# MLP products of a two-layer trunk with both activation parts as one 512-column moving operand

## Chip, cores and metric

The kernel runs on one core of a Trainium2 chip. The metric is the device time of one execution in microseconds (us). The profiler records one execution; times of instructions come from it.

## What is computed

The input is 256 tokens of width 2048 and there are two layers. A layer has a mixer part (input projection, retention, forgetting attention, mLSTM, output projection) and an MLP. The change touches the MLP:

```python
h = rmsnorm(x, norm_mlp_w[layer]) * (1.0 + sc_m) + sh_m
x = x + g_m * (jnp.square(jax.nn.relu(h @ w_ff1[layer])) @ w_ff2[layer])
```

`w_ff1` is 2048 x 8192 and `w_ff2` is 8192 x 2048, all in float32. `sh_m`, `sc_m` and `g_m` come from a matrix-vector product of a condition with `ada_w` (the "ada" work below).

## The kernel before

**Layout.** Activations lie transposed: a tile holds 128 features on the partitions and the 256 tokens along the free axis. The normalised input of a layer part is 16 such tiles (k = 0 to 15).

**Products in parts.** A float32 product is made of three products of rounded parts. A weight tile w is split into a high part wh (a cast on ACT, L221) and a low part wl = w - wh (a subtraction on DVE or POOL, L227); activations are split the same way into hh and hl (L499, L500), and the product is the sum of wh x hl, wl x hh and wh x hh. In `mm_b` (L252 to L254) the weight part is the stationary operand (128 x 128) and an activation part is the moving operand (256 columns), so each pair of k and 128-column block n takes three matmuls with three weight loads, all into the same 256 columns of PSUM. This document calls such a group of three a triple. In `mm_a` (L263 to L265), which makes the v, g and o blocks of the input projection, the activations are stationary and 512 weight columns move.

**Weights.** `chunk` loads a 4 x 128 x 512 piece of a weight matrix as two DMAs of 128 x 1024 values (512 KB each, six buffers `raw`), and `split` makes wh and wl of each (three buffers each). A tile therefore holds two k by four n. `pool_share` is the share of the low parts made on POOL: 0.3 and 0.8 in the two passes of the first ff1 stage of layer 0, 0.8 in the rest of its MLP, and 0 in layer 1.

**PSUM.** `pair` gives a tile of 1024 columns (two banks); there are two of them. An ff1 or ff2 block of 512 outputs fills one pair: four n of 256 columns.

**The MLP.** `ff1` makes a block of 512 hidden features from 16 k tiles. ACT evicts it with a relu (L964), squares it (L969) and casts it to the high part (L971); DVE makes the low part (L972). `ff2` takes two such blocks (8 k tiles) at a time and adds four output blocks of 512 to x, each evicted by four DVE instructions (`residual`, L796). The program order is ff1 of step s, then ff2 of step s - 1, for s = 0 to 7. In layer 0 the first six ff1 blocks are made in two passes over 8 k each (the partial sum is kept in SBUF, L952 and L960), because the modulation of the upper k tiles comes later. The first block of a layer's ff1 is a "lead" (`lead`, L471 to L473): it uses 258 columns of an unnormalised input, so that it can start ahead of the norm. The last output block of layer 1 is made in four small pieces (`ff2_tail`).

**Order of the work.** Each engine and SP's DMA queue runs its instructions in a fixed order that a scheduler with a timeline model chose. The ada work is spread over the MLP by `step`: each ada tile is two DMAs and two DVE products of 128 x 1024 (L283), so that in layer 0 weight DMAs and ada DMAs alternate in SP's queue, and DVE's order mixes ada products with subtractions and evictions.

The lines that the change and the prediction touch:

```python
out += [(hi[:, i, :], lo[:, i, :]) for i in range(step)]          # chunk: a tile holds 2 k x 512 columns
nc.tensor.matmul(o, lhsT=wh[:, s], rhs=al, ...)                   # mm_b, three per (k, n)
nc.tensor.matmul(o, lhsT=wl[:, s], rhs=ah, ...)
nc.tensor.matmul(o, lhsT=wh[:, s], rhs=ah, ...)
```

## Time and profile before

| what | value |
|---|---|
| median of 3 runs | 2548.88 us (2541.46 to 2551.96) |
| the profiled execution | 2549.75 us |
| its span, first to last instruction | 2548.0 us |
| mean granted TensorE clock | 0.977 |
| instructions | 46455 |

Time around the span is 2549.75 - 2548.0 = 1.75 us. In the profile PE is the matmul, PEld the weight load, DVE is VectorE, ACT is ScalarE, POOL is GpSimd, and SP issues the DMAs. Matmuls are pipelined: a matmul's own duration overlaps the next one's, so the cost of one matmul in a stream is the distance from its start to the next start. "Granted clock" 1.00 is TensorE at 2.4 GHz.

### The profile page before, as it was taken

To read this page: it belongs to the slowest core of one execution; us is meant where nothing else is said; L and a number is where in the kernel's file an instruction comes from. 1 tells how busy PE (TensorE), PEld (TensorE's weight loads), DVE (VectorE), ACT (ScalarE), POOL (GpSimd) and SP (SyncE) were. 2 spreads that over 40 slices of the span, in tenths; PEclk is the share of its full clock that TensorE was granted. 3 is DMA by queue.
4 is the path that set the end of the run, shared out by engine and by line. 5 is a ranking of instruction groups with operands and counts; after the bars stand their busy time and mean duration, and the time that the engine had idled before them with its cause. 6 is when DMAs were issued, how large, how long until landed. Compare 5 with 4: busy or idle time off the path is not lost.

```text
span 2548.0 us, 46455 instructions
## 1 busy us (share of the span) xinstructions
PE 2450.1 (96%) x19016; PEld 2378.3 (93%) x19016; DVE 1583.2 (62%) x2427; ACT 1180.9 (46%) x1442; POOL 758.9 (30%) x314
## 2 busy tenths in 40 slices
...
GB/s 359 299 327 329 305 217 265 285 299 338 322 334 310 279 288 297 287 280 298 285 213 241 272 247 266 192 166 178 178 182 186 188 182 183 187 185 183 186 187 91
DMA packets 177246, 630.45 MB, mean 247 GB/s; under 512 B 19588, under 2 KB 24326, under 8 KB 177032
## 3 DMA queue, kind: packets, MB, share of 16 engines
...
q10 hardware_dynamic: 432, 0.39, 0.1%
...
## 4 chain that ended last, share of the span: by engine, by line
PE 79%; DVE 9%; DMA 4%; issue 3%; POOL 3%; ACT 2%; SPq 0%; DVEq 0%; POOLq 0%; ACTq 0%
PE pj L253 23%; PE pj L252 23%; PE pj L254 23%; DMA ada<-ada_w 3%; POOL wl L227 3%; DVE ada L283 2%; PE pj L264 2%; PE pj L265 2%; PE pj L263 2%; DVE wl L227 2%; PE mx L620 1%; ACT wh L221 1%; DVE cv L709 1%; DVE blk L437 0%; DMA raw<-ada_w 0%
## 5 line engine op out<-in xcount | busy, mean ns | idle before, releaser
L221 ACT CAST wh<-raw 128x1024 fp32r<-128x1024 f32 x804 | 840.4, 1047 | 1129.8 <-PE pj L254 881.3
L227 POOL TENSOR_TENSOR wl<-raw,wh 128x1024 fp32r<-128x1024 f32 (+1 forms) x309 | 756.3, 2451 | 583.4 <-ACT wh L221 565.3
L227 DVE TENSOR_TENSOR wl<-raw,wh 128x1024 fp32r<-128x1024 f32 x495 | 615.7, 1246 | 487.4 <-ACT wh L221 486.7
L252 PE MATMUL pj<-hl,wh 128*128 128x256 f32 x2912 | 830.9, 286 | 9.5 <-DVE hl L500 8.2
L253 PE MATMUL pj<-hh,wl 128*128 128x256 f32 x2912 | 830.4, 285 | 7.2 <-DVE wl L227 7.2
L254 PE MATMUL pj<-hh,wh 128*128 128x256 f32 x2912 | 828.1, 284 | 0.0
L253 PE MATMUL pj<-blk,wl 128*128 128x256 f32 x2528 | 713.6, 282 | 6.6 <-DVE wl L227 5.2
L252 PE MATMUL pj<-blk,wh 128*128 128x256 f32 x2528 | 712.8, 282 | 2.8 <-ACT blk L538 1.5
L254 PE MATMUL pj<-blk,wh 128*128 128x256 f32 x2528 | 711.3, 281 | 0.0
L283 DVE SCALAR_TENSOR_TENSOR ada<-ada,cond 128x1024 f32<-128x1024 f32 x380 | 456.7, 1214 | 227.7 <-DMA ada<-ada_w 225.6
L252 PEld LDWEIGHTS pj<-hl,wh 128*128 128x128 f32 x2912 | 561.8, 193 | 10.7 <-DVE hl L500 8.9
L253 PEld LDWEIGHTS pj<-hh,wl 128*128 128x128 f32 x2912 | 562.4, 193 | 9.3 <-DVE wl L227 8.7
L254 PEld LDWEIGHTS pj<-hh,wh 128*128 128x128 f32 x2912 | 562.1, 193 | 0.2
L253 PEld LDWEIGHTS pj<-blk,wl 128*128 128x128 f32 x2528 | 478.5, 189 | 7.3 <-DVE wl L227 5.6
L252 PEld LDWEIGHTS pj<-blk,wh 128*128 128x128 f32 x2528 | 478.8, 190 | 3.4 <-ACT blk L538 1.9
L254 PEld LDWEIGHTS pj<-blk,wh 128*128 128x128 f32 x2528 | 479.3, 190 | 0.0
L1045 POOL TENSOR_TENSOR blk<-blk,R 128x1024 f32<-128x1024 f32 x1 | 2.4, 2357 | 1199.1 <-ACT R L405 1199.1
L264 PE MATMUL pj<-wl,hh 128*128 128x512 f32 x384 | 155.4, 405 | 8.5 <-DVE wl L227 8.4
L796 DVE SCALAR_TENSOR_TENSOR X<-pj,mod,X 128x256 f32<-128x256 f32 x284 | 117.8, 477 | 64.0 <-PE pj L254 63.9
L263 PE MATMUL pj<-wh,hl 128*128 128x512 f32 x384 | 153.2, 399 | 1.2 <-ACT wh L221 1.2
L265 PE MATMUL pj<-wh,hh 128*128 128x512 f32 x384 | 152.9, 398 | 0.0
L264 PEld LDWEIGHTS pj<-wl,hh 128*128 128x128 f32 x384 | 73.7, 192 | 24.5 <-DVE wl L227 10.7
...
## 6 DMA issues: line engine op xcount, KB each, us to landing
...
```

The costliest lines, as they stand in the source:

```text
L221: nc.scalar.copy(hi, raw)
L227: eng.tensor_tensor(lo, raw, hi.bitcast(F32), ALU.subtract)
L252: nc.tensor.matmul(o, lhsT=wh[:, s], rhs=al, start=st, stop=False, skip_group_check=True)
L253: nc.tensor.matmul(o, lhsT=wl[:, s], rhs=ah, start=False, stop=False, skip_group_check=True)
L254: nc.tensor.matmul(o, lhsT=wh[:, s], rhs=ah, start=False, stop=last, skip_group_check=True)
L263: nc.tensor.matmul(o, lhsT=al[:, s], rhs=wh, start=first, stop=False)
L264: nc.tensor.matmul(o, lhsT=ah[:, s], rhs=wl, start=False, stop=False)
L265: nc.tensor.matmul(o, lhsT=ah[:, s], rhs=wh, start=False, stop=last)
L283: nc.vector.scalar_tensor_tensor(raw, raw, 1.0, self.cond, ALU.mult, ALU.mult, accum_out=self.part[l][:, i, h:h + 1])
L620: nc.tensor.matmul(ps[:, i * P:i * P + P], lhsT=lt, rhs=v[:, j, c:c + P], start=first, stop=last, skip_group_check=True)
L709: V.scalar_tensor_tensor(y[:, s:], x[:, n, :T - s], w[:, 3 - s:4 - s], y[:, s:], ALU.mult, ALU.add)
L796: V.scalar_tensor_tensor(self.X(k), ps[:, n * T:n * T + T], self.mod[l][:, c:c + 1], self.X(k), ALU.mult, ALU.add)
```

## The change

The high and low parts of the activations become one tile, `h[:, k]` (or the two halves of a hidden tile), so that wh meets both in one matmul of 512 columns, and wl meets the high part in one of 256 columns. The 512-column result lies in one PSUM bank as two halves, wh x high (+ wl x high) and wh x low, which are added at eviction. A pair of banks now holds two n instead of four. `w_ff1` and `w_ff2` are laid out in blocks of 256 columns; a weight tile is one DMA of four k by 256 columns, of the same size as before. relu and square become one DVE instruction. The lead takes its weights from two such tiles per four k.

```diff
--- before.py
+++ after.py
@@ -116,8 +116,7 @@
     def constants(self):
         nc, c, io = self.nc, self.const, self.io
         self.Xq = [self.acts.tile([P, 4, T], F32, name=f"X{i}") for i in range(4)]
-        self.hh = self.acts.tile([P, KT, T], F32R, name="hh")
-        self.hl = self.acts.tile([P, KT, T], F32R, name="hl")
+        self.h = self.acts.tile([P, KT, 2, T], F32R, name="h")
         self.vec = c.tile([P, DEPTH * NVEC + KT], F32, name="vec")
         nc.scalar.dma_start(self.vec, io["vec"])
         crow = c.tile([2, 1024], F32, name="crow")
@@ -241,6 +240,31 @@
             out += [(hi[:, i, :], lo[:, i, :]) for i in range(step)]
         return out
 
+    def chunk2(self, src):
+
+        raw = self.raw.tile([P, 4, 256], F32, tag="raw", name=self.name("raw"))
+        self.wdma.append(self.nc.sync.dma_start(raw, src))
+        hi, lo = self.split(raw, 4, 256)
+        return [(hi[:, i, :], lo[:, i, :]) for i in range(4)]
+
+    def mm_w(self, ps, w, act, first, last):
+
+
+        nc = self.nc
+        wh, wl = w
+        for n in range(2):
+            s = slice(n * P, n * P + P)
+            o = ps[:, n * 512:n * 512 + 512]
+            nc.tensor.matmul(o.rearrange("p (a b) -> p a b", b=T), lhsT=wh[:, s], rhs=act, start=first, stop=False,
+                             skip_group_check=True)
+            nc.tensor.matmul(o[:, :T], lhsT=wl[:, s], rhs=act[:, 0, :], start=False, stop=last, skip_group_check=True)
+
+    @staticmethod
+    def sums(ps):
+
+        v = ps.rearrange("p (n c) -> p n c", c=512)
+        return v[:, :, 0:T], v[:, :, T:2 * T]
+
     def mm_b(self, ps, w, act, first, last):
 
         nc = self.nc
@@ -457,25 +481,37 @@
             if c == stat_at[1]:
                 self.stat_spread(aux)
             nk = min(4, kts[-1] + 1 - k0)
-            w = self.chunk(wsrc(k0, nk), nk)
+            w = wsrc(k0, nk)
             if js == 3:
                 self.step(nk / 4)
             for k in range(k0, k0 + nk):
                 if k not in self.U:
                     self.lead_u(l, js, jc, [k, k + 1])
-                (wh, wl), (uh, ul) = w[k - k0], self.U.pop(k)
+                uh, ul = self.U.pop(k)
                 f, e = k == kts[0], k == kts[-1]
                 for n in range(4):
-                    s = slice(n * P, n * P + P)
+                    wh, wl = w(k - k0, n)
                     o = ps[n][:, :LT]
-                    nc.tensor.matmul(o, lhsT=wh[:, s], rhs=ul, start=f, stop=False)
-                    nc.tensor.matmul(o, lhsT=wl[:, s], rhs=uh, start=False, stop=False)
-                    nc.tensor.matmul(o, lhsT=wh[:, s], rhs=uh, start=False, stop=e)
+                    nc.tensor.matmul(o, lhsT=wh, rhs=ul, start=f, stop=False)
+                    nc.tensor.matmul(o, lhsT=wl, rhs=uh, start=False, stop=False)
+                    nc.tensor.matmul(o, lhsT=wh, rhs=uh, start=False, stop=e)
         if self.r is None:
             self.stat_sum(aux)
         if self.R is None:
             self.stat_spread(aux)
         return ps
+
+    def lead_win(self, l):
+        def get(k, nk):
+            w = self.chunk(self.io["w_in"][l, 0, k // 4][:, k % 4:k % 4 + nk, :], nk)
+            return lambda i, n: tuple(x[:, n * P:n * P + P] for x in w[i])
+        return get
+
+    def lead_ff1(self, l):
+        def get(k, nk):
+            w = [self.chunk2(self.io["w_ff1"][l, b, k // 4]) for b in range(2)]
+            return lambda i, n: tuple(x[:, n % 2 * P:n % 2 * P + P] for x in w[n // 2][i])
+        return get
 
     def lead_out(self, ps, dst, func=AF.Identity, scale=1.0):
         nc = self.nc
@@ -496,11 +532,12 @@
                 s = js * KT + k + i
                 nc.scalar.activation(t[:, i, :], t[:, i, :], AF.Identity,
                                      scale=self.mod[l][:, c:c + 1], bias=self.mod[l][:, s:s + 1])
-            nc.scalar.copy(self.hh[:, k:k + 2, :], t)
-            nc.vector.tensor_tensor(self.hl[:, k:k + 2, :], t, self.hh[:, k:k + 2, :].bitcast(F32), ALU.subtract)
+            hi, lo = self.h[:, k:k + 2, 0, :], self.h[:, k:k + 2, 1, :]
+            nc.scalar.copy(hi, t)
+            nc.vector.tensor_tensor(lo, t, hi.bitcast(F32), ALU.subtract)
 
     def hact(self, k):
-        return self.hh[:, k, :], self.hl[:, k, :]
+        return self.h[:, k, 0, :], self.h[:, k, 1, :]
 
 
     def gate_mm(self, l):
@@ -842,7 +879,7 @@
             self.pump_until(l, 0, kts[-1])
             led = g == 0 and cfg["lead_win"]
             if led:
-                ps = self.lead(l, 0, 1, lambda k, n: io["w_in"][l, 0, k // 4][:, k % 4:k % 4 + n, :], kts, cfg["stat_win"])
+                ps = self.lead(l, 0, 1, self.lead_win(l), kts, cfg["stat_win"])
             if l > 0:
                 self.h_make(l, 0, 1, kts)
             if led:
@@ -911,15 +948,13 @@
             led = g == 0
             self.rate(cfg["ada_ff1"][g], nb * len(kts) / 4)
             if led:
-                ps = self.lead(l, 3, 4, lambda k, n: io["w_ff1"][l, 0, k // 4][:, k % 4:k % 4 + n, :], kts, cfg["stat_ff1"])
+                ps = self.lead(l, 3, 4, self.lead_ff1(l), kts, cfg["stat_ff1"])
             self.h_make(l, 3, 4, kts)
             if led:
                 acc[0] = self.slot()
+                self.lead_out(ps, acc[0])
                 if kts[-1] == KT - 1:
-                    self.lead_out(ps, acc[0], AF.Relu)
                     acc[0] = self.square(acc[0])
-                else:
-                    self.lead_out(ps, acc[0])
             for b in range(1 if led else 0, nb):
                 acc[b] = self.ff1(l, b, kts, acc.get(b))
         self.pool_share = cfg["pool_ff"]
@@ -937,63 +972,63 @@
 
     def ff1(self, l, b, kts, acc=None):
         nc = self.nc
-        ps = self.pair()
-        for k0 in range(kts[0], kts[-1] + 1, 4):
-            nk = min(4, kts[-1] + 1 - k0)
-            r0 = k0 % 4
-            w = self.chunk(self.io["w_ff1"][l, b, k0 // 4][:, r0:r0 + nk, :], nk)
-            for i in range(nk):
-                k = k0 + i
-                self.mm_b(ps, w[i], self.hact(k), k == kts[0], k == kts[-1])
-            self.step(nk / 4)
-        if kts[-1] != KT - 1:
-            if acc is None:
-                acc = self.slot()
-                nc.scalar.copy(self.flat(acc), ps)
+        done = kts[-1] == KT - 1
+        fresh = acc is None
+        t = self.slot() if fresh else acc
+        for h in range(2):
+            ps = self.pair()
+            for k0 in range(kts[0], kts[-1] + 1, 4):
+                w = self.chunk2(self.io["w_ff1"][l, 2 * b + h, k0 // 4])
+                for k in range(k0, k0 + 4):
+                    self.mm_w(ps, w[k - k0], self.h[:, k], k == kts[0], k == kts[-1])
+                self.step(0.5)
+            d = t[:, 2 * h:2 * h + 2, :]
+            p0, p1 = self.sums(ps)
+            if fresh:
+                nc.scalar.copy(d, p1)
             else:
-                d = self.flat(acc)
-                nc.vector.tensor_tensor(d, ps, d, ALU.add)
-            return acc
-        if acc is not None:
-            t = acc
-            d = self.flat(t)
-            nc.vector.tensor_tensor(d, ps, d, ALU.add)
-            nc.scalar.activation(t, t, AF.Relu)
-        else:
-            t = self.slot()
-            nc.scalar.activation(self.flat(t), ps, AF.Relu)
-        return self.square(t)
+                nc.vector.tensor_tensor(d, p1, d, ALU.add)
+            nc.vector.tensor_tensor(d, p0, d, ALU.add)
+        return self.square(t) if done else t
 
     def square(self, t):
-        nc = self.nc
-        nc.scalar.activation(t, t, AF.Square)
-        hi, lo = self.slot(dt=F32R), self.slot(dt=F32R)
-        nc.scalar.copy(hi, t)
-        nc.vector.tensor_tensor(lo, t, hi.bitcast(F32), ALU.subtract)
-        return hi, lo
+
+        nc = self.nc
+        nc.vector.scalar_tensor_tensor(t, t, 0.0, t, ALU.max, ALU.mult)
+        out = []
+        for h in range(2):
+            s = self.slot((P, 2, 2, T), F32R)
+            nc.scalar.copy(s[:, 0], t[:, 2 * h:2 * h + 2, :])
+            nc.vector.tensor_tensor(s[:, 1], t[:, 2 * h:2 * h + 2, :], s[:, 0].bitcast(F32), ALU.subtract)
+            out.append(s)
+        return lambda i: out[i // 2][:, :, i % 2, :]
 
     def ff2(self, l, s, hid, last):
+        V = self.nc.vector
         if last:
             self.stat_begin()
         tail = last and l == DEPTH - 1
-        for nb in range(3 if tail else 4):
+        for nb in range(6 if tail else 8):
+            if last and nb >= 6:
+                self.early(CFG[l + 1]["early_win"], nb - 6, l + 1, 0, 1)
             ps = self.pair()
             for c in range(2):
-                if nb == 3 and last:
-                    self.early(CFG[l + 1]["early_win"], c, l + 1, 0, 1)
-                w = self.chunk(self.io["w_ff2"][l, nb, 2 * s + c], 4)
-                hi, lo = hid[c]
+                w = self.chunk2(self.io["w_ff2"][l, nb, 2 * s + c])
                 for i in range(4):
-                    self.mm_b(ps, w[i], (hi[:, i, :], lo[:, i, :]), c == 0 and i == 0, c == 1 and i == 3)
-                self.step()
-            self.residual(l, 5, nb, ps)
-            if last:
-                self.stat_piece(nb)
-                if nb == 3:
+                    self.mm_w(ps, w[i], hid[c](i), c == 0 and i == 0, c == 1 and i == 3)
+                self.step(0.5)
+            for n in range(2):
+                k = 2 * nb + n
+                g = self.mod[l][:, 5 * KT + k:5 * KT + k + 1]
+                for c in range(n * 512, n * 512 + 512, T):
+                    V.scalar_tensor_tensor(self.X(k), ps[:, c:c + T], g, self.X(k), ALU.mult, ALU.add)
+            if last and nb % 2 == 1:
+                self.stat_piece(nb // 2)
+                if nb == 7:
                     self.early(CFG[l + 1]["early_win"], 2, l + 1, 0, 1)
             if tail:
-                for n in range(4):
-                    self.final_scale(4 * nb + n)
+                for n in range(2):
+                    self.final_scale(2 * nb + n)
         if tail:
             self.ff2_tail(l, s, hid)
 
@@ -1005,13 +1040,13 @@
             raw = self.raw.tile([P, 8, P], F32, tag="raw", name=self.name("raw"))
             for c in range(2):
                 nc.sync.dma_start(raw[:, 4 * c:4 * c + 4, :],
-                                  self.io["w_ff2"][l, 3, 2 * s + c][:, :, n * P:n * P + P])
+                                  self.io["w_ff2"][l, 6 + n // 2, 2 * s + c][:, :, n % 2 * P:n % 2 * P + P])
             wh, wl = self.split(raw, 8, P)
             for i in range(8):
-                ah, al = hid[i // 4][0][:, i % 4, :], hid[i // 4][1][:, i % 4, :]
-                nc.tensor.matmul(ps, lhsT=wh[:, i, :], rhs=al, start=i == 0, stop=False)
-                nc.tensor.matmul(ps, lhsT=wl[:, i, :], rhs=ah, start=False, stop=False)
-                nc.tensor.matmul(ps, lhsT=wh[:, i, :], rhs=ah, start=False, stop=i == 7)
+                a = hid[i // 4](i % 4)
+                nc.tensor.matmul(ps, lhsT=wh[:, i, :], rhs=a[:, 1, :], start=i == 0, stop=False)
+                nc.tensor.matmul(ps, lhsT=wl[:, i, :], rhs=a[:, 0, :], start=False, stop=False)
+                nc.tensor.matmul(ps, lhsT=wh[:, i, :], rhs=a[:, 0, :], start=False, stop=i == 7)
             k = 12 + n
             x = self.X(k)
             nc.vector.scalar_tensor_tensor(x, ps, self.mod[l][:, 5 * KT + k:5 * KT + k + 1], x, ALU.mult, ALU.add)
@@ -1061,10 +1096,10 @@
     return np.swapaxes(v.reshape(*v.shape[:-1], -1, P), -1, -2)
 
 
-def _chunks(w):
+def _chunks(w, n=512):
 
     L, K, N = w.shape
-    return np.ascontiguousarray(w.reshape(L, K // 512, 4, P, N // 512, 512).transpose(0, 4, 1, 3, 2, 5))
+    return np.ascontiguousarray(w.reshape(L, K // 512, 4, P, N // n, n).transpose(0, 4, 1, 3, 2, 5))
 
 
 def _layout(inp):
@@ -1082,7 +1117,7 @@
     g[:, :, R_MI:R_MI + 4] = w_in[:, :, COL_MI:COL_MI + 4]
     a["w_gate"] = np.ascontiguousarray(g.reshape(DEPTH, KT, P, NG).transpose(0, 2, 1, 3))
     for k in ("w_out", "w_ff1", "w_ff2"):
-        a[k] = _chunks(inp[k])
+        a[k] = _chunks(inp[k], 512 if k == "w_out" else 256)
     vec = np.zeros((P, DEPTH * NVEC + KT), np.float32)
     for l in range(DEPTH):
         v = vec[:, l * NVEC:(l + 1) * NVEC]
```

## Rows read from the trace of the kernel before

**Rows 1.** The profile's page: busy time of each engine; chain that ended last by engine.

```profile
PE 2450.1 (96%) x19016; PEld 2378.3 (93%) x19016; DVE 1583.2 (62%) x2427; ACT 1180.9 (46%) x1442; POOL 758.9 (30%) x314
...
PE 79%; DVE 9%; DMA 4%; issue 3%; POOL 3%; ACT 2%; SPq 0%; DVEq 0%; POOLq 0%; ACTq 0%
```

**Rows 2.** Busy time by stretch, whole MLP stages; columns as the first row says.

```profile
core 0: us, PE busy (x) PEld busy (x) DVE busy (x) ACT busy (x) POOL busy (x), PEclk, DMA share, GB/s
...
600.00:1300.00 700.00, 698.68 (x5861) 698.30 (x5859) 359.13 (x546) 312.08 (x313) 463.47 (x189) 1.00 0.85 301
1813.30:2510.00 696.70, 695.17 (x5837) 694.76 (x5837) 373.95 (x399) 313.76 (x325) 0.00 (x0) 1.00 0.55 183
```

**Rows 3.** The same view: one ff1 step and one ff2 step of layer 1.

```profile
2021.50:2067.50 46.00, 46.00 (x386) 46.00 (x385) 22.31 (x21) 19.54 (x19) 0.00 (x0) 1.00 0.55 184
2067.50:2113.00 45.50, 45.50 (x387) 45.50 (x386) 25.43 (x29) 19.57 (x19) 0.00 (x0) 1.00 0.56 185
```

**Rows 4.** Timeline of PE, layer 1, end of 512-column stretch: start us, us, instruction.

```profile
1692.17 0.39 PE L265 MATMUL pj<-wh,hh 128*128 128x512 f32 x1
...
1695.35 0.39 PE L264 MATMUL pj<-wl,hh 128*128 128x512 f32 x1
1695.57 0.39 PE L265 MATMUL pj<-wh,hh 128*128 128x512 f32 x1
1695.80 0.28 PE L252 MATMUL pj<-blk,wh 128*128 128x256 f32 x1
1695.92 0.28 PE L253 MATMUL pj<-blk,wl 128*128 128x256 f32 x1
1696.04 0.28 PE L254 MATMUL pj<-blk,wh 128*128 128x256 f32 x1
```

**Rows 5.** Timeline of PE, layer 0, a 512-column stretch.

```profile
102.16 0.40 PE L263 MATMUL pj<-wh,hl 128*128 128x512 f32 x1
...
103.09 0.39 PE L264 MATMUL pj<-wl,hh 128*128 128x512 f32 x1
```

**Rows 6.** Costliest groups of instructions: form, count | busy us, mean ns | idle before.

```profile
L252 PE MATMUL pj<-hl,wh 128*128 128x256 f32 x2912 | 830.9, 286 | 9.5 <-DVE hl L500 8.2
L252 PE MATMUL pj<-blk,wh 128*128 128x256 f32 x2528 | 712.8, 282 | 2.8 <-ACT blk L538 1.5
```

**Rows 7.** Groups by line, DVE and ACT.

```profile
L796 DVE SCALAR_TENSOR_TENSOR X<-pj,mod,X 128x256 f32<-128x256 f32 x284 | 117.8, 477 | 64.0 <-PE pj L254 63.9
L972 DVE TENSOR_TENSOR blk<-blk,blk 128x1024 fp32r<-128x1024 f32 x32 | 56.0, 1751 | 29.3 <-ACT blk L971 29.3
L969 ACT ACTIVATE blk<-blk 128x1024 f32<-128x1024 f32 x32 | 33.9, 1061 | 0.1
L964 ACT ACTIVATE blk<-pj 128x1024 f32<-128x1024 f32 x25 | 25.6, 1026 | 45.4 <-PE pj L254 45.4
L499 ACT CAST hh<-ht 128x512 fp32r<-128x512 f32 x24 | 14.4, 614 | 0.2
L500 DVE TENSOR_TENSOR hl<-ht,hh 128x512 fp32r<-128x512 f32 x24 | 16.1, 685 | 1.4 <-ACT hh L499 1.3
```

**Rows 8.** Line 227 in 600 to 1300 us: durations ns minimum/median/maximum, and who waited.

```profile
L227 POOL TENSOR_TENSOR wl<-raw,wh x189: 2380/2403/3381, 604.5 to 1299.7; 128x1024 fp32r<-128x1024 f32 x189
L227 DVE TENSOR_TENSOR wl<-raw,wh x54: 1211/1224/2117, 599.6 to 1286.5; 128x1024 fp32r<-128x1024 f32 x54
...
  PE pj L253: 1.4, 1
```

**Rows 9.** Busy time by stretch: lead of layer 0, second ff1 pass, lead of layer 1.

```profile
640.00:700.00 60.00, 60.00 (x503) 60.00 (x502) 41.27 (x47) 36.68 (x37) 40.40 (x16) 1.00 0.92 319
552.00:580.00 28.00, 22.00 (x140) 21.65 (x141) 26.94 (x55) 14.39 (x28) 2.38 (x1) 0.76 0.85 296
1789.00:1813.40 24.40, 24.40 (x208) 24.40 (x207) 18.57 (x39) 14.83 (x23) 0.00 (x0) 1.00 0.52 172
```

**Rows 10.** Groups of DVE in 650 to 700 us.

```profile
L972 DVE TENSOR_TENSOR blk<-blk,blk 128x1024 fp32r<-128x1024 f32 x4 | 10.3, 2587 | 7.7 <-ACT blk L971 7.7
...
L960 DVE TENSOR_TENSOR blk<-pj,blk 128x1024 f32<-128x1024 f32 x4 | 4.9, 1222 | 4.7 <-PE pj L254 4.7
```

**Rows 11.** Waits in 600 to 1250 us: total us, times, longest us.

```profile
DVE ada L283 <- DMA ada<-ada_w: 165.3, 46, 8.9
```

**Rows 12.** Timeline of DVE: the first and last of 25 long ada waits.

```profile
837.30 1.22 DVE L283 SCALAR_TENSOR_TENSOR ada<-ada,cond 128x1024 f32<-128x1024 f32 x1 [6.78 <-DMA ada<-ada_w]
...
1255.99 1.22 DVE L283 SCALAR_TENSOR_TENSOR ada<-ada,cond 128x1024 f32<-128x1024 f32 x1 [6.82 <-DMA ada<-ada_w]
```

## Prediction

> **What bounds the kernel now.** I read the page first: PE is busy 96% of the span, and 79% of the chain that ended last is PE [rows 1]. PE busy alone proves little here, since matmuls overlap, so I then read the two MLP stages by stretch: PE has work in 698.7 of 700 us in layer 0 and in 695.2 of 696.7 us in layer 1, at a granted clock of 1.00 (its 2.4 GHz level), while DVE is at 51% and 54%, POOL at 66% in layer 0 and the DMA engines at 0.85 and 0.55 [rows 2]. So the MLP is bound by how close together matmuls start, and a change pays here by changing that distance. One ff1 step in layer 1 is two blocks of 16 x 4 x 3, 384 matmuls, in 46.0 us; one ff2 step is four blocks of 8 x 4 x 3, also 384, in 45.5 us [rows 3] (the rows count two or three at the edges besides). That is 120 ns and 118.4 ns for 256 columns. 256 columns at 2.4 GHz are 106.7 ns, so 12 to 13 ns of each matmul are not columns. Does the rest grow with the columns or come once per matmul? The 512-column matmuls of the input projection answer: from 1692.17 to 1695.80 us there are 16 starts, 3.63 / 16 = 227 ns each, against 213.3 ns of columns: 13.6 ns over, the same as for 256. The next matmul of 256 columns follows the last 512 after 230 ns (rounded to 10) and then the old distance of 120 ns returns [rows 4]. So the rest comes once per matmul with its weight load, and the two widths can follow each other at no price.
>
> **What the change removes.** A triple has the same 768 columns before and after, in two matmuls instead of three. Triples: ff1 has 16 blocks x 16 k x 4 n = 1024 per layer, less those of the lead (32 in layer 0, 64 in layer 1), so 1952; ff2 has 8 x 4 x 8 x 4 = 1024 per layer, less 32 of the tail, so 2016. The counts agree with the groups: 2912 on hl is 1952 + 960 of the input projection, 2528 on blk is 2016 + 512 of the output projection [rows 6].
> - ff1: 3 x 120 = 360 ns becomes 227 + 120 = 347 ns; 13.0 ns x 1952 = 25.4 us.
> - ff2: 3 x 118.4 = 355.2 becomes 227 + 118.4 = 345.4; 9.8 ns x 2016 = 19.8 us.
>
> Together 45.2 us. Bounds: in layer 0 four 512-column starts take 0.93 us, 232.5 ns [rows 5]; by that a triple saves 7.5 and 4.3 ns, 23 us in all. At the other end, if the 1.6 ns by which ff2 is quicker than ff1 go to its 512 as well (and to ff1's pairs by the shared tile), 2016 x 1.6 + 1952 x 1.6 more, 51.5 us. I take 45.2, since the 227 ns are from a stretch of layer 1 in which, as in the MLP, PE waits for nothing.
>
> TensorE: Matmul & The Clock Gate in the Trainium skill (section Back-to-back issue gap) gives N / 2.4 + 2.5 ns for a warm matmul: 109 ns for 256 and 216 ns for 512. By it the change would save 2.5 ns x 3968, 10 us. The trace disagrees with the constant (120 and 227 ns) and agrees with the slope.
>
> **What it adds or moves.**
> - *Weight tiles.* A tile is now 4 k x 2 n, still 8 (k, n) pairs, one DMA of the same 512 KB, one cast, one subtraction: the counts on SP, ACT, DVE and POOL stay, and so do the steps of ada work (half a step, twice as often). A tile lasts PE 8 x 345 = 2.76 us instead of 2.84. Cost nothing; the cover is the two other tiles: 5.5 us less a cast of 1.05 and a subtraction of 2.40 on POOL or 1.22 on DVE [rows 8], so 2 and 3.2 us.
> - *The lead.* Its k takes 12 x 0.12 = 1.44 us and now needs two tiles for four k, of three buffers. The second tile of the next four k can only be cast when the first of these is released, 0.72 us before their end; 1.05 + 1.22 and hand-offs are 2.4 us, and it is wanted 1.44 us after the release: 1.0 us late, or 2.2 with POOL. Three such places in layer 1, one in layer 0, and at each start one tile more before n = 2. The layer 1 lead runs closed up now (PE 24.4 of 24.4 us), layer 0's is held by DVE (26.9 of 28.0 us) [rows 9]. I take 5 us between 0 and 10.
> - *ff1 evictions.* Per block ACT loses a relu (1.03 us) and a square (1.06), keeps the cast as two halves (0.61 each) and gains two copies of 512 columns; DVE gains two sums of 512 columns (0.69 each by the 128x512 subtraction), one relu-square of 1024 (1.2 as the other 1024-wide forms) and keeps the low part [rows 7, 8, 10]: some 2.6 us a block. In most of the MLP that lies beside PE: layer 1 gets 15 x 2.6 = 39 us on DVE. The second pass of layer 0 (about 640 to 710 us) is different: DVE is busy 41.3 of 60 us there [rows 9], a block takes 11.5 us, each now has four sums for one of 1.22 us (+1.5) and the relu-square (+1.2, or 2.6 if POOL slows it as it slows L972: 2587 ns there against a mean of 1751 [rows 7, 10]). With 5.2 blocks that is 14 to 21 us more, 55 to 63 us of work in a stretch that should shrink to 58. Bounds 0 and 22 us; I take 4, since only the upper half of that load exceeds the stretch.
> - *ff2 evictions.* A pair of banks fills in 8 x 2 x 345 ns = 5.5 us instead of 11.4, and its four DVE instructions still take 4 x 0.48 = 1.9 us [rows 7]. DVE gets 252 more, 120 us over both layers, beside PE. But the cover of a late eviction falls from 9.5 to 3.6 us, and in layer 0 DVE stands waiting for ada DMAs 46 times, 165 us in all and up to 8.9 us [rows 11]; 25 of these waits lie between 3.2 and 8.9 us, of which two are shown [rows 12], and they sum to 147 us, 57 us beyond 3.6 each. What is queued behind them is the eviction and DVE's share of the subtractions. Today's subtractions on DVE have a cover no better (3.2 us) behind the same waits, and PE lost 1.4 us to them in 700 [rows 8]: the order keeps urgent work ahead of these waits. So I take 3 us, between 0 and 57.
> - *DMA.* The same bytes in less time: 0.85 in layer 0 becomes 0.88. Nothing. *Tail.* Same work in the same order: nothing.
>
> **Sum.** -45.2 + 5 + 4 + 3 = -33. Made against the profiled execution, 2549.75 us, this gives 2516.5; that execution stands 0.9 us over the median of the runs.
>
> **Rivals.**
> - *The constant does not go.* If the 13 ns belonged to the 256 columns streamed (or a 512-wide matmul were run as two halves, with a moving operand in ff2 that is two separate runs of 256), a triple would cost the same as before, and only the costs of 0 to 12 us remain: 2550 to 2562. For it: no 512-column matmul here has its two halves apart, and none is seen between 256s. Against: 227 ns [rows 4], in a stream where each matmul has its own weights. By the skill's constant (above) the time would be 2549.75 - 10 + 12 = 2552, which is this case. Chance 0.08.
> - *Layer 0 gives all back.* There DVE and POOL slow each other: L972 takes 2587 ns, and POOL's subtraction goes from 2403 up to 3381 ns [rows 8, 10], which eats half of its 2 us of cover. If the new DVE work makes this the pace of layer 0, only layer 1 gains: 960 x 13.0 + 992 x 9.8 = 22.2 us less 3 for its lead, 2531. Against: POOL is at 66% over the stage. SBUF — State Buffer in the Trainium skill (section Who interferes with whom) says that a DVE instruction with two SBUF inputs and a GpSimd instruction that reads SBUF exclude each other; the stretched rows agree, and the relu-square is such an instruction. Chance 0.12.
> - *Slower: evictions behind the ada waits.* In ff2 of layer 0, an eviction queued on DVE behind an ada product that waits for its DMA stops PE once the wait is over 3.6 us. If every long wait stood so, it would cost 57 us (beyond the cover) to 147 us (whole); from 48 us on (45.2 - 9 + 12) the kernel is slower by over 0.5%. At 70 us: 2549.75 - 45.2 + 9 + 70 = 2584. For it: the cover shrinks to under half. Against: the subtractions' record. Chance 0.06.
>
> **The numbers.** Forecast as worked out: 0.72, 2516.5, by itself 2498 (-51.5 and no costs) to 2540 (the low saving of 23 us with the costs taken gives 2539). With layer 0's case the range 2498 to 2540 holds 0.82; 0.02 is left for more than that gain. About 0.5%, 12.7 us, is what a measurement of this kernel can tell from no change: faster is below 2536, slower above 2562. Faster: 0.70 + 0.10 + 0.02 = 0.82. Slower: 0.06 + 0.02 of the first rival. Same: 0.10.
>
> **What the profile after would show.** Right: in the MLP of layer 1 starts 227 ns after a 512 and 120 ns after a 256, a step of ff1 in 44.4 us and one of ff2 in 44.2; 3968 matmuls fewer on PE; PE never waiting for an eviction. The lead of layer 1 some 3 us longer; DVE near full in 640 to 710 us. Wrong: 240 ns after a 512 (first rival); PE waiting for wl from POOL in layer 0 (second); PE waiting for DVE's evictions, with long ada waits ahead of them (third). A saving well above 50 us would mean that weight loads, and not a fixed rest, set the 120 ns.

## The result and the profile after

| | before | after |
|---|---|---|
| median, us (7 runs each) | 2547.27 (2538.67 to 2551.96) | 2564.57 (2556.41 to 2572.14) |
| profiled execution, us | 2549.75 | 2566.22 |
| its span, us | 2548.0 | 2564.4 |

The ratio is 1.0062, 95% interval 1.0043 to 1.0081: the change made the kernel slower by 0.6%, against a forecast of 1.3% faster. 2564.57 lies outside the range.

The page of after (busy time; chain by engine; groups: form, count | busy, mean ns | idle before):

```profile
PE 2429.6 (95%) x15048; PEld 2175.5 (85%) x15048; DVE 1805.2 (70%) x2821; ACT 1152.1 (45%) x1466; POOL 759.2 (30%) x314
...
PE 74%; DVE 12%; DMA 7%; issue 4%; ACT 1%; POOL 1%; SPq 1%; DVEq 0%; POOLq 0%; ACTq 0%
...
L258 PE MATMUL pj<-blk,wh 128*128 128x512 f32 x2016 | 714.4, 397 | 17.4 <-DVE X L1024 17.4
L258 PE MATMUL pj<-h,wh 128*128 128x512 f32 x1952 | 692.1, 399 | 12.3 <-DVE blk L991 7.2
```

The counts are the predicted ones (2016 and 1952 triples, 3968 matmuls fewer than in [rows 1]). New is what stands at the right end of the last two rows: the first matmul of a block now waits for DVE's evictions, L1024 of ff2 and L991 of ff1. The groups of before at the same place had no such releaser [rows 6]. DVE went from 62 to 70% of the span, and its share of the chain from 9 to 12%.

Where the time went is read by parts of the span, cut at the same instructions of PE in both traces: the end of layer 0's lead, the start and end of the lead of layer 1's input projection (that stretch is called the boundary below), the end of layer 1's ff1 lead, the start of the tail.

| part, us | before | after | difference |
|---|---|---|---|
| start to the end of layer 0's lead | 561.3 | 560.8 | -0.5 |
| MLP of layer 0 | 739.3 | 759.8 | +20.5 |
| boundary (unchanged code) | 39.8 | 44.3 | +4.5 |
| rest of layer 1 up to its MLP | 472.8 | 474.6 | +1.8 |
| MLP of layer 1 | 696.6 | 688.1 | -8.5 |
| tail to the end | 38.2 | 36.8 | -1.4 |

So layer 1 gains and layer 0 loses. The last two cuts are not quite the same place: in before 23 matmuls of ff2's last block, some 2.7 us, stand behind the tail's first matmul, in after none. By the same work layer 1's MLP is some 11 us shorter and the tail some 1 us longer.

These parts come from the one profiled execution of each kernel, while the seven executions of after spread over 16 us. Two programs also differ in parts that no edit touches: over all the runs below, the first part takes 551 to 562 us. A difference of a few us in one part is therefore not a finding by itself.

Busy time by stretch of the three stretches that matter, first in before, then in after:

```profile
561.30:1300.60 739.30, 728.93 (x6077) 727.78 (x6075) 398.12 (x602) 336.29 (x355) 469.68 (x192) 0.99 0.85 300
1300.60:1340.40 39.80, 32.33 (x226) 31.93 (x227) 25.55 (x43) 13.31 (x19) 20.67 (x9) 0.83 0.57 196
1813.20:2509.80 696.60, 695.07 (x5836) 694.66 (x5835) 374.05 (x399) 313.77 (x324) 0.00 (x0) 1.00 0.55 183
```

```profile
560.80:1320.60 759.80, 726.42 (x4073) 631.29 (x4072) 526.14 (x806) 317.46 (x365) 472.91 (x192) 0.98 0.81 291
1320.60:1364.90 44.30, 32.03 (x220) 31.00 (x218) 29.60 (x50) 13.38 (x19) 18.66 (x9) 0.85 0.54 180
1839.50:2527.60 688.10, 685.04 (x3907) 597.21 (x3906) 465.17 (x585) 305.38 (x341) 0.00 (x0) 1.00 0.55 185
```

In layer 0 PE is without work in 33.4 us (759.80 less 726.42) where it was in 10.4, and DVE is busy 526 of 760 us (69%) where it was 398 of 739 (54%). In layer 1 DVE is as full (465 of 688, 68%), and PE still has work in all but 3 us. DVE's load alone, as a share of the time, is therefore not what stops PE.

From the starts of PE's matmuls I use one more measure below: **open time**, the sum of the distances of over 0.45 us between two starts, less 0.23 us each (a 512-column matmul). In layer 0's MLP it is 11.0 us in 7 places before and 36.4 us in 25 places after; in layer 1's 1.5 and 3.2 us.

What PE waited for in 560 to 1320 us and in 1290 to 1366 us of after (total us, times, longest us):

```profile
PE pj L258 <- DVE X L1024: 17.4, 9, 5.1
PE pj L258 <- DVE blk L991: 7.2, 4, 4.7
```

```profile
PE pj L407 <- DVE ss L399: 7.0, 1, 7.0
PE pj L495 <- DVE X L1024: 5.2, 1, 5.2
```

And DVE's order around the longest of these waits, from its timeline (start us, us, instruction):

```profile
1128.90 2.33 DVE L997 SCALAR_TENSOR_TENSOR blk<-blk 128x1024 f32<-128x1024 f32 x1
1131.91 4.96 DVE L1002 TENSOR_TENSOR blk<-blk,blk 128x512 fp32r<-128x512 f32 x2 [0.69 <-ACT blk L1001]
1136.80 1.21 DVE L307 SCALAR_TENSOR_TENSOR ada<-ada,cond 128x1024 f32<-128x1024 f32 x1
1137.93 0.08 DVE L307 DVE_READ_ACCUMULATOR ada<-ada,cond 128x1 f32 x1
1137.93 0.47 DVE L1024 SCALAR_TENSOR_TENSOR X<-pj,mod,X 128x256 f32<-128x256 f32 x1
1138.33 1.20 DVE L307 SCALAR_TENSOR_TENSOR ada<-ada,cond 128x1024 f32<-128x1024 f32 x1
1139.47 0.08 DVE L307 DVE_READ_ACCUMULATOR ada<-ada,cond 128x1 f32 x1
1139.47 0.87 DVE L1024 SCALAR_TENSOR_TENSOR X<-pj,mod,X 128x256 f32<-128x256 f32 x2
1140.26 2.15 DVE L226 TENSOR_TENSOR wl<-raw,wh 128x1024 fp32r<-128x1024 f32 x1
1142.32 1.78 DVE L1024 SCALAR_TENSOR_TENSOR X<-pj,mod,X 128x256 f32<-128x256 f32 x4
```

From 1131.9 to 1142.8 DVE has no pause. It makes two low parts of a hidden block (2.48 us each; POOL works at that time, and a DVE subtraction of that shape takes 0.69 us in [rows 7]), two ada products, a weight's low part (2.15 us, against a median of 1.22 in [rows 8]), and the four evictions of one block lie scattered among them: one, two, and the first of the last four. On PE the other block was complete at 1137.6, and its next matmul started at 1142.94, when that fourth eviction was done. No ada DMA is waited for in these 11 us. It is so in the other long waits too: DVE is busy 5.00 of 5.00 us in 585 to 590 us and 4.96 of 5.00 in 1235 to 1240.

Such a wait costs more than itself. Three stretches of after, the wait, what follows and the normal state (after the sum of each engine: the granted clock):

```profile
1137.00:1143.00 6.00, 0.94 (x7) 0.61 (x5) 6.00 (x10) 1.04 (x1) 2.35 (x1) 0.80 0.73 263
1143.00:1148.00 5.00, 5.00 (x17) 4.27 (x18) 3.83 (x8) 0.01 (x1) 0.00 (x0) 0.56 0.59 210
1148.00:1160.00 12.00, 12.00 (x70) 10.52 (x69) 5.30 (x10) 4.95 (x5) 7.21 (x3) 1.00 0.53 181
```

After 5.3 us without matmuls the granted clock is at its lower level (1.2 GHz) for most of 5 us: 17 matmuls there, against 29 at the rate of the third row. Five such stretches follow waits in layer 0's MLP (from 590.1, 699.7, 1142.9, 1239.8 and 1310.4 us), 18.9 us with work at half rate, so some 9 us lost. Before had none between 580 and 1300 us (clock 1.00; from 600 us on in [rows 2]). The Trainium skill, page TensorE: Matmul & The Clock Gate, section HAM oscillation — how this bites in real kernels, prices time at the lower clock at half its length; 17 against 29 matmuls agrees roughly.

### The profile page after: what moved, and what is told of

The parts are those of the page before. It is cut to its first block, busy times and chain, and to the rows that moved or that the text cites. A ratio compares the mean times of both kernels' runs of the same rounds, so it can differ in the third digit from the quotient of the medians.

```text
span 2564.4 us, 38950 instructions
## 1 busy us (share of the span) xinstructions
PE 2429.6 (95%) x15048; PEld 2175.5 (85%) x15048; DVE 1805.2 (70%) x2821; ACT 1152.1 (45%) x1466; POOL 759.2 (30%) x314
## 4 chain that ended last, share of the span: by engine, by line
PE 74%; DVE 12%; DMA 7%; issue 4%; ACT 1%; POOL 1%; SPq 1%; DVEq 0%; POOLq 0%; ACTq 0%
PE pj L258 31%; PE pj L260 16%; PE pj L277 5%; PE pj L276 5%; PE pj L278 5%; DMA ada<-ada_w 5%; DVE ada L307 3%; DVE wl L226 3%; PE pj L288 2%; PE pj L289 2%; PE pj L287 2%; POOL wl L226 1%; DVE blk L1002 1%; DVE blk L997 1%; DMA raw<-w_in 1%
## 5 line engine op out<-in xcount | busy, mean ns | idle before, releaser
L258 PE MATMUL pj<-blk,wh 128*128 128x512 f32 x2016 | 714.4, 397 | 17.4 <-DVE X L1024 17.4
L258 PE MATMUL pj<-h,wh 128*128 128x512 f32 x1952 | 692.1, 399 | 12.3 <-DVE blk L991 7.2
L260 PE MATMUL pj<-blk,wl 128*128 128x256 f32 x2016 | 569.6, 283 | 0.4 <-POOL wl L226 0.4
L260 PE MATMUL pj<-h,wl 128*128 128x256 f32 x1952 | 549.9, 282 | 1.2 <-POOL wl L226 0.6
L258 PEld LDWEIGHTS pj<-blk,wh 128*128 128x128 f32 x2016 | 381.9, 189 | 108.7 <-issue 16.2
L258 PEld LDWEIGHTS pj<-h,wh 128*128 128x128 f32 x1952 | 368.7, 189 | 102.5 <-DVE blk L991 6.2
L260 PEld LDWEIGHTS pj<-h,wl 128*128 128x128 f32 x1952 | 371.2, 190 | 1.8 <-POOL wl L226 0.9
L1024 DVE SCALAR_TENSOR_TENSOR X<-pj,mod,X 128x256 f32<-128x256 f32 x504 | 231.1, 480 | 91.1 <-PE pj L260 86.1
L276 PE MATMUL pj<-h,wh 128*128 128x256 f32 x960 | 277.6, 289 | 7.9 <-DVE h L537 6.8
L277 PE MATMUL pj<-h,wl 128*128 128x256 f32 x960 | 276.8, 288 | 6.6 <-DVE wl L226 6.6
L278 PE MATMUL pj<-h,wh 128*128 128x256 f32 x960 | 274.8, 286 | 0.0
L277 PEld LDWEIGHTS pj<-h,wl 128*128 128x128 f32 x960 | 186.8, 195 | 8.7 <-DVE wl L226 8.1
L276 PEld LDWEIGHTS pj<-h,wh 128*128 128x128 f32 x960 | 186.7, 195 | 8.8 <-DVE h L537 6.9
L278 PEld LDWEIGHTS pj<-h,wh 128*128 128x128 f32 x960 | 186.7, 195 | 0.2
L288 PE MATMUL pj<-wl,h 128*128 128x512 f32 x384 | 155.6, 405 | 12.1 <-DVE wl L226 12.1
L287 PE MATMUL pj<-wh,h 128*128 128x512 f32 x384 | 153.0, 399 | 1.2 <-ACT wh L220 1.2
## 6 DMA issues: line engine op xcount, KB each, us to landing
raw<-ada_w SPq DMA_DIRECT2D x4, 512.0 KB, 10.4
```

Of the source, the lines that this page charges most:

```text
L258: nc.tensor.matmul(o.rearrange("p (a b) -> p a b", b=T), lhsT=wh[:, s], rhs=act, start=first, stop=False, skip_group_check=True)
L260: nc.tensor.matmul(o[:, :T], lhsT=wl[:, s], rhs=act[:, 0, :], start=False, stop=last, skip_group_check=True)
L276: nc.tensor.matmul(o, lhsT=wh[:, s], rhs=al, start=st, stop=False, skip_group_check=True)
L277: nc.tensor.matmul(o, lhsT=wl[:, s], rhs=ah, start=False, stop=False, skip_group_check=True)
L278: nc.tensor.matmul(o, lhsT=wh[:, s], rhs=ah, start=False, stop=last, skip_group_check=True)
L287: nc.tensor.matmul(o, lhsT=al[:, s], rhs=wh, start=first, stop=False)
```

## The experiments

All but run 10 are built from the kernel after. The expectations name causes by letters. **A**: evictions that wait on DVE hold PE up (**A1**: behind work that keeps DVE busy; **A2**: behind ada products that wait for their DMA, the form in which the prediction had it as a rival). **C**: the cover of an eviction, the time by which it may be late, has become too short. **D**: the new DVE work and POOL slow each other. **E**: the time from the last matmul of a block to the release of its banks decides (run 7). **F**: the distance after a 512-column matmul depends on its neighbours (run 6, where G is the rival that it does not). In run 5 alone, C means something else: a loss in layer 1 or between the two MLPs. "L0" is the length of layer 0's MLP.

| run | edit | median us | ratio to before | L0 us | open us | boundary us | layer 1 MLP us |
|---|---|---|---|---|---|---|---|
| before | | | | 739.3 | 11.0 | 39.8 | 696.6 |
| after | | 2564.57 | 1.0062 | 759.8 | 36.4 | 44.3 | 688.1 |
| 1 | 512 as 2 x 256 | 2566.38 | 1.0086 | 766.1 | 29.0 | 32.9 | 701.2 |
| 2 | one half evicted | 2519.69 | 0.9892 | 733.2 | 16.2 | 34.9 | 687.8 |
| 3 | short ada products | 2509.89 | 0.9858 | 725.2 | 10.7 | 33.9 | 688.7 |
| 4 | square on ACT | 2528.41 | 0.9928 | 739.0 | 22.5 | 28.6 | 688.9 |
| 5 | layer 1 only | 2540.66 | 0.9977 | 743.4 | 13.4 | 39.3 | 686.9 |
| 6 | 512s in a row | 2550.95 | 1.0014 | 759.2 | 37.7 | 33.4 | 686.2 |
| 7 | ACT takes a half | 2540.27 | 0.9973 | 751.8 | 29.9 | 33.1 | 687.5 |
| 8 | 4 and 7 | 2531.25 | 0.9940 | 745.3 | 25.2 | 33.3 | 688.5 |
| 9 | 4, old ff2 in layer 0 | 2539.28 | 0.9972 | 738.9 | 19.8 | 40.6 | 687.2 |
| 10 | before, DVE square | 2549.61 | 1.0002 | 744.9 | 14.4 | 40.6 | 696.7 |
| 11 | ada steps behind | 2545.92 | 0.9997 | 753.7 | 31.0 | 34.3 | 687.6 |
| 12 | 4 and 11 | 2540.51 | 0.9973 | 744.6 | 24.7 | 33.4 | 688.9 |
| 13 | third pair in ff2 | 2538.29 | 0.9969 | 743.0 | 26.1 | 34.7 | 688.7 |
| 14 | 4 and 13 | 2530.89 | 0.9937 | 734.3 | 19.8 | 33.5 | 688.9 |

The intervals of these ratios are between 0.0009 and 0.0023 to either side. Each ratio is to runs of before that were taken together with that run (medians 2545.37 to 2547.27 us). Parts and open time are those of the profiled execution.

Read a run by L0 and open time first, not by its median. The boundary is 44.3 us in after and 28.6 to 34.9 in every run that keeps the new ff2 in layer 0, so every such edit of after gained 9 to 16 us there. The section on the prediction says why.

### 1. What the wide matmul itself is worth

```
-  matmul(o[:, 0:512], wh, rhs=act)                       # both halves
+  matmul(o[:, :T], wh, rhs=act[:, 0, :]); matmul(o[:, T:], wh, rhs=act[:, 1, :])
```

> Undoes the 512-column matmul alone: wh meets the high and the low part in two matmuls of 256 columns again, with the weight tiles, PSUM halves and evictions of the changed kernel kept. Theory A (512 columns pay on PE, late evictions on DVE in layer 0 take it back): the distance of a triple goes back from about 351 to 355 to 360 ns, 5.5 to 6.5 ns x 3968 = 24 us more; evictions get a little more cover, so some of the 33 us of waits in layer 0 may go. Time 2575 to 2590 us against 2565 for the changed kernel. Rival B (the wide matmul itself, or PE reading two halves, is what costs): the time falls to 2555 or below.

Measured: 1.0086 [1.0066, 1.0107]. Slower than after, as A had it, but by 2 us where 10 to 25 were expected. The two MLPs together are 1435.9 us before (some 1438.6 with the matmuls behind the cut), 1467.3 in this run and 1447.9 after. So all that the change does besides the wide matmul costs some 29 us in the MLPs, and the wide matmul takes 19 of them back: 13 in layer 1 and 6 in layer 0, where open time is 7 us less here. In the time of the whole run only some 2 us of the 19 show, because two stretches of unchanged code were shorter here than in after, the boundary by 11.4 us and the rest of layer 1 by 7.4.

### 2 and 3. Is it DVE's evictions, and what stands ahead of them?

Run 2 leaves the product of wh with the low part out of the result (the second half is summed but never evicted). Run 3 takes only 64 of the 1024 columns of each ada product in layer 0's MLP, so that part of the modulation is left out; the DMAs stay.

```
-  V.scalar_tensor_tensor(X(k), ps[:, c:c + T], ...) for both halves     # run 2 (ff1 likewise)
+  the first half only
-  nc.vector.scalar_tensor_tensor(raw, raw, 1.0, cond, ...)              # run 3
+  nc.vector.scalar_tensor_tensor(raw[:, :64], raw[:, :64], 1.0, cond[:, :64], ...)
```

> Leaves the half wh x low out at eviction (it is still computed by PE), so that DVE has half of the ff2 evictions and one of two sums in ff1; PE's work is the same. Theory A: PE's waits for DVE's evictions in layer 0's MLP fall from some 25 us to under 8, and the time to 2533 to 2545 us, below the kernel before. Rival B (the pair of banks is simply too small, or the new weight tiles or POOL hold PE): PE still waits 20 us or more in layer 0, time 2557 us or above.

> In layer 0's MLP the ada products on DVE read 64 of 1024 columns (the rest is left out); their DMAs, their places in DVE's order and all evictions stay. Theory A1 (an eviction stands behind busy DVE work: ada products, low parts, subtractions): PE's waits for evictions in layer 0 fall below 8 us, time 2530 to 2545 us. Theory A2, the form that was predicted (an eviction stands behind an ada product that waits for its DMA): the DMAs land as before, so 20 us or more of PE's waits stay and the time is 2555 us or above.

Measured: 0.9892 [0.9869, 0.9914] and 0.9858 [0.9840, 0.9876]. Both are quicker than any range of their expectations. Without the second half's evictions the kernel is 45 us quicker than after, and PE's waits for evictions in layer 0's MLP fall from 24.6 to 2.3 us, as A had it; 27 of the 45 us are that MLP, 9 the boundary, and the rest other stretches. Run 3 parts A1 from A2, because it shortens DVE's work and leaves its DMA waits. In 600 to 1290 us DVE waited for ada DMAs, in after and in run 3:

```profile
DVE ada L307 <- DMA ada<-ada_w: 117.2, 56, 7.1
```

```profile
DVE ada L309 <- DMA ada<-ada_w: 117.0, 56, 8.1
```

The same 56 waits and 117 us. But what PE waited for in run 3 (551 to 1277 us) shrank from 17.4 and 7.2 us to

```profile
PE pj L259 <- DVE X L1028: 2.6, 1, 2.6
...
PE pj L259 <- DVE blk L995: 0.8, 1, 0.8
```

So in layer 0's MLP the evictions stand behind work that keeps DVE busy, not behind its waits for DMAs: A1 holds there and A2 falls. L0 is 34.6 us shorter than in after; the rest of the gain is the boundary (10.4) and other stretches. The groups of DVE in 600 to 1290 us of after show which work that is:

```profile
L307 DVE SCALAR_TENSOR_TENSOR ada<-ada,cond 128x1024 f32<-128x1024 f32 x154 | 186.3, 1215 | 117.7 <-DMA ada<-ada_w 117.2
L1024 DVE SCALAR_TENSOR_TENSOR X<-pj,mod,X 128x256 f32<-128x256 f32 x232 | 106.2, 480 | 47.8 <-PE pj L260 45.0
L226 DVE TENSOR_TENSOR wl<-raw,wh 128x1024 fp32r<-128x1024 f32 x53 | 70.1, 1322 | 24.8 <-ACT wh L220 23.8 <-DMA raw<-w_ff 0.7
L1002 DVE TENSOR_TENSOR blk<-blk,blk 128x512 fp32r<-128x512 f32 x32 | 46.0, 1466 | 4.8 <-ACT blk L1001 4.8
L997 DVE SCALAR_TENSOR_TENSOR blk<-blk 128x1024 f32<-128x1024 f32 x16 | 37.5, 2344 | 0.4
L991 DVE TENSOR_TENSOR blk<-pj,blk 128x512 f32<-128x512 f32 x40 | 27.5, 686 | 26.3 <-ACT blk L988 26.1
```

### 5. Layer 1 alone

```
   def ff1 / ff2 / square:  if l == 0, the form of before (512-column chunks, three matmuls of 256)
```

> The changed form in layer 1 only; layer 0's MLP as before the change. Theory A (the loss is in layer 0, where DVE also has the ada work): 960 x 6.5 + 992 x 5.5 ns = 11.7 us of saving remain with no waits, 2533 to 2540 us against 2547 before, so both kernels are beaten. Rival C (a part of the loss comes with the change in layer 1, or in the mixer between the two MLPs, 6 us longer after the change): 2543 us or above.

Measured: 0.9977 [0.9964, 0.9989]. Layer 1's MLP takes 686.9 us, 9.7 less than before (some 12 by the same work), and layer 0's 743.4 us, in the form of before and yet 4 us longer than in before. The time misses A's range by 0.7 us and the rival's by 2.3. The new form is a gain where there is no ada work and POOL has none (layer 1), and after's loss is in layer 0's MLP and the boundary behind it.

### 6. Does the distance depend on the neighbours?

```
-  512(n=0) 256(n=0) 512(n=1) 256(n=1)
+  512(n=0) 512(n=1) 256(n=0) 256(n=1)
```

> Per k the two 512-column matmuls are issued first and then the two of 256 columns, instead of in turn; nothing else. Theory F (a 512 that follows a 256 costs 4 to 8 ns more than one that follows a 512): a pair of matmuls falls from 349 to 355 ns to 345 to 348, and the time by 10 to 20 us. Rival G (the distance has to do with the operands or the banks and not with the neighbour): the sum of a pair stays within 2 ns, the time within 5 us of the changed kernel.

Measured: 1.0014 [1.0004, 1.0025]. The mean of a triple is 348 ns in ff1 and 350 in ff2 of layer 1 (351 and 350 in after), and the start after a 512 comes after a mean of 232 to 233 ns whether a 256 or another 512 follows. F falls. Both MLPs are nearly as in after (759.2 and 686.2 us). The time fell by 14 us, into F's range, by luck: in the profiled executions 11 us of the difference are the boundary (33.4 against 44.3) and 4 the stretch ahead of layer 0's MLP.

### 4, 7 and 8. Less work on DVE

```
-  nc.vector.scalar_tensor_tensor(t, t, 0.0, t, ALU.max, ALU.mult)      # 4: relu and square
+  nc.scalar.activation(t, t, AF.Relu); nc.scalar.activation(t, t, AF.Square)
-  four V.scalar_tensor_tensor(X(k), ps[...], g, X(k)) a block          # 7: ff2's eviction
+  nc.scalar.copy(u, low halves); V.tensor_tensor(u, high halves, u); two V.scalar_tensor_tensor(X(k), u, g, X(k))
```

> relu and square of ff1 go back to ACT (two instructions), as before the change; all else of the changed kernel stays. DVE loses one instruction of 1024 columns per ff1 block, 37.5 us in 600 to 1290 us. Theory A1 (an eviction stands behind DVE's busy work of all kinds): the 36 us that PE stands open in layer 0's MLP fall by a share, to 20 to 30 us, and the time to 2548 to 2558. Rival D (it is above all the work with two SBUF operands, which POOL and DVE make longer for each other): they fall below 15 us, time 2535 to 2548.

> In ff2 ACT copies the half wh x low of a pair of banks to SBUF and DVE adds the other half to it (512 columns, 0.69 us); the two products into x are then made from SBUF. The banks are free after some 1.3 us of two engines instead of 1.9 us of DVE, and DVE has 1.65 us per pair instead of 1.9. Theory E (the time from the last matmul of a pair to its release decides): PE's waits for ff2 evictions fall below 8 us, time 2538 to 2553. Theory A1 in its plain form (what stands ahead of an eviction in DVE's order decides): they stay at 12 us or more, time 2553 to 2565.

> Both of the two edits above together, which take DVE's work in layer 0's MLP down by some 37 + 16 us. Theory A1: PE stands open for 15 to 22 us in layer 0's MLP, time 2538 to 2550. If the two edits help in the same waits, no better than the better one of them.

Measured: run 4 0.9928 [0.9913, 0.9942], run 7 0.9973 [0.9964, 0.9983], run 8 0.9940 [0.9921, 0.9958]. In run 4 DVE is busy 497 us in layer 0's MLP, where it was 526 in after, and PE's open time falls from 36.4 to 22.5 us, as A1 had it; it is the quickest complete form found, 36 us below after and 18 below before. That is below both ranges, because the boundary gave 15.7 of the 36 us and L0 20.8. Run 7 is as E had it: moving half of ff2's eviction to ACT takes PE's waits for ff2's evictions from 17.4 to 7.5 us (L0 -8.0 us). But the two do not add: run 8 is no better than run 4, and its open time is no smaller. PE still waits 8.0 us for ff2's evictions and 4.7 for ff1's there (9.6 and 5.1 in run 4). Run 8 puts the relu, the square and the copies on ACT, which also makes every weight's high part; what makes those evictions late was not separated.

### 10. Is it the kind of instruction that was added?

```
 (kernel before)
-  nc.scalar.activation(t, t, AF.Relu) ... nc.scalar.activation(t, t, AF.Square)
+  nc.vector.scalar_tensor_tensor(t, t, 0.0, t, ALU.max, ALU.mult)
```

> The kernel before, with relu and square as one VectorE instruction in place of two of ScalarE; no wide matmul, no halves. Theory C (the new form's cost is the short cover of the evictions, which is unchanged here): within 8 us of the kernel before, open time in layer 0's MLP 11 to 18 us. Rival D (the cost is the VectorE instruction with two SBUF operands, which competes with GpSimd): 15 us or more slower, open time in layer 0's MLP at 25 us or more.

Measured: 1.0002 [0.9987, 1.0017]. The relu-square takes a mean of 1749 ns on DVE there, but with the old blocks, whose evictions may be 9.5 us late, it costs nothing that can be measured in the time of the kernel, and open time (14.4 us) lies where C had it. (L0 is 5.6 us longer than before, in the slowest of the run's ten executions.) D falls as a cause by itself. Whether POOL has a share in the cost where the cover is short was not tested: no run takes POOL's work out of after.

### 9. The old ff2 in layer 0

```
 (run 4)  def ff2:  if l == 0, the form of before: 512-column chunks, three matmuls of 256, four slices a block
```

> Relu and square are two ScalarE instructions, and ff2 of layer 0 alone is as before (three matmuls of 256 columns, 512-column weight chunks, one eviction instruction for a pair of slices); the rest is the new form. Theory C (what an eviction may be late by decides: the old ff2 of layer 0 gives 9.5 us of matmuls for 4.7, and pays for it with about 12 us of closed time): layer 0's MLP about 730 us against 739 of the run with the square on ScalarE, open time in it at most 14 us against 22.5, 2515 to 2525 us. Rival (the wide form of ff2 in layer 0 pays as much as it costs, and the open time sits in ff1): 2528 to 2540 us, open time at or above 20 us.

Measured: 0.9972 [0.9960, 0.9985], slower than run 4. A miss of C's number, and the rival's range: L0 is the same as in run 4 (738.9 and 739.0 us). PE's waits for ff2's evictions are gone (9.6 us in run 4), as C had it, but others take their place: 4.9 us for the low parts of weights from DVE and POOL, and 1.4 for a high part from ACT. Open time falls by only 2.7 us, and the rest of L0, where the old matmuls cost more, grows by as much. The 11 us to run 4 are the boundary, 40.6 against 28.6 us.

### 11 and 12. What stands ahead in the program

```
-  self.step(0.5)      # inside the block's loop, ahead of its evictions
+  self.step(0.5)      # behind the block's evictions (ff1 and ff2); run 12 with the edit of run 4 too
```

> The kernel after, with the calls that hand out ada work moved behind the evictions in ff1 and ff2, so that ada products are emitted after the eviction that they stood ahead of. Theory A1 (an eviction waits for the VectorE work that stands ahead of it in its queue): open time in layer 0's MLP falls from 36 us to under 22 us, 2540 to 2555 us. Rival (the order on VectorE does not follow the order of emission closely enough, or the backlog is there whatever stands last): open time 30 us or more, 2560 to 2570 us.

> The run before this one with relu and square as two ScalarE instructions. If both edits act on the same cause and add up: open time in layer 0's MLP under 16 us, 2515 to 2525 us. If the order of emission changes nothing: as the run with the square on ScalarE alone, 2525 to 2532 us and about 22 us open.

Measured: 0.9997 [0.9984, 1.0009] and 0.9973 [0.9959, 0.9987]. Open time fell only from 36.4 to 31.0 us, so the order on DVE follows the emission loosely, as the rival has it. The time (2545.92) lies in the range of A1 all the same, but for another reason: in the profiled executions, 22 us apart, 10 are the boundary, 6 L0 and 4 the stretch ahead of it. With the square on ACT the step order costs 12 us (run 12 against run 4), and run 12 is slower than both ranges of its expectation. The order of emission is no lever here.

### 13 and 14. The cover alone

```
-  ps = self.pair()                                     # ff2: two pairs of PSUM banks in turn
+  ps = [self.bank(), self.bank()] if nb % 3 == 2 and not last else the two halves of self.pair()
```

Every third block of ff2 uses two banks that stand idle there. The matmuls, the evictions and DVE's work stay.

> The kernel after, but in ff2 (all steps but the last of a layer) every third block sums into two PSUM banks of the pool that is otherwise idle there, so that a block's evictions may be late by two blocks (about 11.2 us) and not by one (5.6 us). The same matmuls, the same evictions, the same VectorE work. Theory (the short cover of an eviction turns VectorE's bursts into open time): TensorE's waits for X in layer 0's MLP fall from 17.4 to under 6 us, open time there from 36 to under 24 us, 2540 to 2552 us. Rival (VectorE is behind by its whole load in layer 0, and one block more of cover fills up as well): waits for X at 12 us or more, 2560 to 2570 us.

> The run before this one with relu and square as two ScalarE instructions. If cover and load add up: open time in layer 0's MLP under 15 us, 2515 to 2524 us. If the load alone was the cause: as the run with the square on ScalarE, 2525 to 2532 us.

Measured: 0.9969 [0.9958, 0.9980], 26 us below after, with the same DVE load: busy time by stretch of layer 0's MLP and the boundary in run 13, and what PE waited for in 560 to 1302 us:

```profile
557.70:1300.70 743.00, 719.17 (x4072) 626.86 (x4072) 526.72 (x805) 317.79 (x365) 474.64 (x192) 0.99 0.82 298
1300.70:1335.40 34.70, 29.46 (x220) 28.61 (x218) 27.12 (x50) 13.35 (x19) 19.22 (x9) 0.90 0.65 221
```

```profile
PE pj L258 <- DVE blk L991: 9.5, 6, 4.7
...
PE pj L258 <- DVE X L1028: 3.3, 3, 2.6
```

DVE is busy 526.7 us, as in after (526.1), and POOL 474.6 (472.9). PE's waits for ff2's evictions go from 17.4 to 3.3 us, and those of ff1, whose cover was not touched, stay (7.2 and 9.5). Open time fell to 26.1 us, 2 us short of the expectation's mark, and the time below its range, since 9.6 of the 26 us are the boundary. L0 is 16.8 us shorter: less open time and less time at the lower clock. So in ff2 the short cover is a cause that runs have shown: more cover takes the waits away under the same load. Run 3 shows the other half: shorter work ahead of the evictions takes them away under the same cover. The waits need both. Run 14 came out in the range of its second case (the load alone, which run 13 excludes) and not as the sum of cover and load: 2530.89 us, with 19.8 us open where under 15 were expected. Its L0 is the shortest of the forms that leave nothing out (734.3 us, 4.7 below run 4), but its median is that of run 4 within the intervals, as its boundary is 5 us longer.

## Why the prediction was wrong

By its own steps:

- **The saving, -45.2 us: mis-sized, about -30.** An ff1 step of layer 1 was to take 44.4 us and an ff2 step 44.2. One ff2 step and two ff1 steps of after, by stretch:

```profile
1911.77:1956.55 44.78, 44.78 (x259) 39.31 (x257) 34.00 (x48) 18.42 (x19) 0.00 (x0) 1.00 0.57 188
2046.40:2090.78 44.38, 44.38 (x259) 38.80 (x257) 25.41 (x26) 19.36 (x21) 0.00 (x0) 1.00 0.57 190
2135.64:2180.84 45.20, 45.20 (x258) 39.18 (x257) 25.41 (x26) 19.39 (x21) 0.00 (x0) 1.00 0.55 186
```

  Of six ff1 steps three take 44.4 us, as predicted, and three 45.2; the six ff2 steps take 44.6 to 45.0. Against 46.06 and 45.45 that is 1.26 and 0.66 us for 128 triples, 9.8 and 5.2 ns each: 19.2 + 10.4 = 29.6 us over all triples. Starts of PE in such a step of ff2:

```profile
2099.76 0.28 PE L260 MATMUL pj<-blk,wl 128*128 128x256 f32 x1
2099.88 0.40 PE L258 MATMUL pj<-blk,wh 128*128 128x512 f32 x1
2100.12 0.28 PE L260 MATMUL pj<-blk,wl 128*128 128x256 f32 x1
2100.24 0.40 PE L258 MATMUL pj<-blk,wh 128*128 128x512 f32 x1
2100.47 0.28 PE L260 MATMUL pj<-blk,wl 128*128 128x256 f32 x1
```

  120 ns after a 256, as said, and 230 to 240 after a 512, where the step took 227 from [rows 4]. The value of layer 0, 232.5 ns [rows 5], which was set aside as a bound, was nearer. Why half of the ff1 steps are slower by 0.8 us is open.
- **ff2 evictions, "I take 3 us, between 0 and 57": the step that failed.** It named the right place and the right number, the cover that falls from 9.5 to 3.6 us, and then argued it away with the subtractions, which have a cover of 3.2 us and lost PE 1.4 us (that one wait was for a subtraction on POOL, so DVE's had lost none). That record did not carry over. A reason that the kernels suggest, and no run tests: a weight's subtraction is one instruction that the scheduler can give to either engine, an eviction is four on DVE alone, all of which must be through. PE waits 17.4 us for them, run 13 gets 14 of these back by giving cover, and the lower clock after the long waits adds up to 9 us for ff1 and ff2 together, a term that the sum did not have. And it looked for the cost in DVE's pauses (the third rival), when what stands ahead of the evictions is busy work.
- **ff1 evictions, "I take 4": also low.** PE waits 7.2 us for L991, 4.7 of them at one place of the first pass (585 us), where the prediction saw no cost, and two of the stretches at the lower clock follow ff1's waits. The DVE load was seen rightly: DVE was said to get 14 to 21 us more in the second pass, and it got 15.3 in 640 to 700 us (41.27 us in [rows 9]):

```profile
640.00:700.00 60.00, 56.16 (x318) 48.22 (x317) 56.56 (x66) 25.18 (x29) 39.24 (x16) 1.00 0.89 316
```

  But the work was summed over a stretch of 58 us, as if it could be late by that much; DVE was not over-full, and PE lost 3.8 us all the same.
- **The lead, +5: too high.** Layer 1's lead takes 24.2 us for 24.1, layer 0's 15.5 for 17.7.
- **Tail and DMA, nothing: right in size.** By the same work the tail took some 1 us more. The DMA share of layer 0's MLP went from 0.85 to 0.81 and not to 0.88, as the stage became longer.
- **What no step had: the boundary.** Its code is unchanged, and it went from 39.8 to 44.3 us, since both the last eviction of layer 0 (5.2 us) and a sum for the norm (7.0; 6.1 before) are late on DVE there. The wait for the sum, 6.1 to 7.0 us, stands in before, after and runs 5, 9 and 10. In these five kernels DVE's order has an ada product, which waits 0.9 to 1.9 us for its DMA, ahead of the norm's last two sums (L398 and L399 in after); in ten of the other eleven both sums come first, and there the wait is under 1 us. DVE's order in after, then in run 4:

```profile
1337.02 1.22 DVE L307 SCALAR_TENSOR_TENSOR ada<-ada,cond 128x1024 f32<-128x1024 f32 x1 [1.84 <-DMA ada<-ada_w]
...
1338.16 1.93 DVE L398 TENSOR_TENSOR ss<-ss,blk 128x512 f32<-128x512 f32 x1
1340.01 5.05 DVE L461 SCALAR_TENSOR_TENSOR blk<-X,mod,blk 128x256 fp32r<-128x256 f32 x2
...
1346.53 0.68 DVE L399 TENSOR_TENSOR ss<-ss,blk 128x512 f32<-128x512 f32 x1
```

```profile
1307.38 0.69 DVE L398 TENSOR_TENSOR ss<-ss,blk 128x512 f32<-128x512 f32 x1
...
1308.38 0.69 DVE L399 TENSOR_TENSOR ss<-ss,blk 128x512 f32<-128x512 f32 x1
1310.22 1.22 DVE L307 SCALAR_TENSOR_TENSOR ada<-ada,cond 128x1024 f32<-128x1024 f32 x1 [0.76 <-DMA ada<-ada_w]
```

  With the wait for the sum the boundary takes 39 to 44 us, without it 33 to 35, and in run 4, which has neither of the two waits, 28.6:

```profile
1299.50:1328.10 28.60, 27.54 (x219) 26.56 (x219) 21.46 (x44) 13.38 (x19) 19.87 (x9) 1.00 0.79 271
```

  So a small edit far away shifts this stretch by up to 16 us through DVE's order. Why the scheduler's order differs there was not found out, and no run moves that ada product alone.

The sum after the fact: about -30 for the triples, +27 for layer 0's open time (25.4, and 0.11 us in each of the 18 places more, since the normal distance at most of them is the 0.12 us after a 256), +9 at the lower clock, +2 open in layer 1, +4.5 at the boundary, and +3 elsewhere: +15.5, against +16.4 between the two spans.

Of the rivals, the first (the constant does not go, nothing saved) is false: both kinds of step of layer 1 became shorter. That its range, up to 2562, ends 3 us from the result is chance. The formula of the Trainium skill that stands beside it (TensorE: Matmul & The Clock Gate, section Back-to-back issue gap) is given there for an isolated matmul and not for a stream with weight loads, so it bears on neither case. The second (layer 0 gives all back, and layer 1 gains) had the right sign in each layer, but not the mechanism: PE waits 1.0 us for POOL's low parts in 560 to 1320 us. POOL may still have a share, by making DVE's work ahead of an eviction longer (2.48 us for a low part, above). The third had the right wait on PE and, in the MLP, the wrong cause on DVE; an ada product that waits for its DMA stood ahead of PE's need at the boundary instead. The chances put 0.08 on slower; the forecast's error was to price a cover that shrinks to two fifths as nearly free.
